# A PEER decoder layer: the second 128 sparse tokens' value rows added on VectorE, and the routing lookups summed over the innermost axis

## The chip, the cores and the metric

The kernel runs on one core of a Trainium2 chip. The metric is device time in microseconds (us) of one execution. A profiled execution gives the trace; its span runs from the first instruction to the last.

## The reference, cut to what matters

One layer over 512 tokens of width 1024. A token mixer comes first (projections, convolutions, pooling, attention, a layer norm); its output `x1` goes into a PEER expert mixer:

```python
q = (xf @ wq).reshape(t, 8, 2, 128)
scores = einsum("thpc,hpnc->thpn", q, sub_keys)
s_top, i_top = lax.top_k(scores, 16)
cand_s = s_top[:, :, 0, :, None] + s_top[:, :, 1, None, :]      # 16 x 16 sums
cand_i = i_top[:, :, 0, :, None] * 128 + i_top[:, :, 1, None, :]
best_s, best_pos = lax.top_k(cand_s, 16)
expert_idx = take_along_axis(cand_i, best_pos)                  # the lookups
act = gelu(einsum("cd,chkd->chk", x, u_tab[expert_idx])) * softmax(best_s)
out = einsum("chk,chkd->cd", act, v_tab[expert_idx])            # 128 rows a token
x = layer_norm(alpha * x + out)
```

Each token has 8 heads with 16 experts, so 128 rows of `u` and 128 rows of `v`, each row 1024 float32 numbers (4 KB). The tables have 16384 rows.

## The kernel before, in words

**Stages.** The mixer fills the first 200 us. Then comes the routing (`route_a` to `route_e`, to about 365 us): for each of 8 heads and two halves, `top16` finds the best 16 on VectorE, and two lookups turn a position among the candidates into the indices of the two halves. A lookup (`lookup`, L789) compares on VectorE (`ge`, float16, 1024 numbers a partition, the axes t, a, s) and multiplies on GpSimd by a difference (`pr`, the same axes); the 16 products of each output are then summed on VectorE. `add_up` (L797, called by `route_d`) sums the float32 products in one `tensor_reduce` whose innermost axis steps by 16 elements; `add_half` (L801, called by `route_e`) sums the float16 products in four `tensor_tensor` adds of halves (512, 256, 128 and 64 outputs). `route_d` and `route_e` work one and two iterations behind `route_c`, in the loop over `hp` (L865), and GpSimd's queue also holds the `wlo` subtractions (`split_w`, L118) that the next query projection on TensorE waits for. While VectorE ends the routing, TensorE works on blocks of the next stage (`ramp_fill`).

**The main loop** (L1267) treats the tokens in two ways. For the last 256 tokens ("dense") it goes through the whole tables, in 128 blocks of 128 experts. A block loads 512 KB of `uT` and 512 KB of `v`, splits each into a high and a low part (ScalarE copies, VectorE subtracts: `wlo`, `vl`), computes `h_run` (24 matmuls), multiplies by gates (`a_mul`, VectorE, L1004) and adds into `acc` (`v_tile`, 12 matmuls a block). The gates come as one-hot products (`g_hot` on VectorE, `g_token` on TensorE) in three windows of blocks, 14 to 31, 38 to 62 and 70 to 94 (`GWIN`), 16 groups in each.

For the first 256 tokens ("sparse", two groups of 128) it gathers rows by indirect DMAs that GpSimd issues (L1037), 128 rows of 4 KB (512 KB) at a time, into a ring of `NGAT` = 9 buffers named `gat`. A *u-row step* (`sparse_u`, L1040, one unit) holds row j of all 128 tokens of a group, a token on each partition, and makes one VectorE multiply with `accum_out`. A *V step* (`sparse_v`, L1097, four units) holds four gathers, in which the partitions are the 128 rows of one token, and makes eight matmuls of 512 columns with `expand` into `facc`; 32 such steps serve a group. The index tile is `idxs[i]` for u and its transpose `idxT` for v.

**Order.** The order of the sparse work is a list written by hand (L1164 to L1192), and `gq` holds the gathers in the same order. `work` (L1204) is called four times in a block and takes from the list by quotas: 5 units a block up to block 13, then 3.5, then about 4 from block 31. So the 128 u-row steps of group 0 run in blocks 0 to 30; then four u-row steps of group 1 alternate with one V step of group 0 (blocks 30 to 93); then group 0 is finished (`finish_a`, `finish_q`, `finish_0`, `finish_1`, block 94), and the 32 V steps of group 1 run, one a block, in blocks 94 to 125. What is left runs behind the loop, with `finish_a(128, ...)` and the last norms.

Each engine works in the order in which the program issues. In block b, TensorE does `h_run(b+1)`, then `v_tile(b)`; VectorE does the split for `b+2`, the split for `b+1`, the gate products, `a_mul(b+1)` (which waits for `h_run(b+1)`), `a_low(b+1)`, and the sparse steps in between. `v_tile(b+1)` waits for `a_low(b+1)`.

## Time and profile before

| | |
|---|---|
| median of 3 runs | 1426.06 us (1424.3 to 1428.26) |
| the profiled execution's own time | 1420.93 us |
| its span | 1419.1 us |
| mean granted TensorE clock | 0.977 |
| TensorE busy | 1322.5 us, 93% |
| VectorE busy | 1086.8 us, 77% |
| GpSimd busy | 779.0 us, 55% |
| ScalarE busy | 512.5 us, 36% |
| moved by DMA | 439.83 MB |

A busy share is a mean over stages with different limits, so the rows below cut the span into stages. PE is TensorE's matmuls, PEld its weight loads, DVE VectorE, ACT ScalarE, POOL GpSimd, SP the queue that issues plain loads. A tile's name is that of the program; a buffer is written left of `<-` and read right of it.

### The profile page before, as it was taken

Reading aid. Unit: us, or ns where it says so; the run is one execution under the profiler, and the core shown is the slowest. Engines: PE = TensorE matmul, PEld = TensorE weight load, DVE = VectorE, ACT = ScalarE, POOL = GpSimd, SP = SyncE. Lnnn points to the kernel's source line nnn. Section 1 sums busy time; section 2 is a strip of 40 time slices with the busy share of each in tenths; the row PEclk is TensorE's granted clock in tenths of the full one; section 3 lists DMA queues with packets and bytes.
Section 4 is the critical chain, followed back from the end, with each engine's and each line's share of the span. In section 5 each row is a group of like instructions: output and inputs, shape, how many; then the busy total and the mean of one; then the engine's idle time right before and its main releaser. Section 6 shows DMA issues by size and latency. Waiting matters only on the chain.

```text
span 1419.1 us, 24250 instructions
## 1 busy us (share of the span) xinstructions
PE 1322.5 (93%) x9229; PEld 1006.2 (71%) x9229; DVE 1086.8 (77%) x2292; ACT 512.5 (36%) x735; POOL 779.0 (55%) x687
## 2 busy tenths in 40 slices
PE   9999999989995668998999999999999989999996
PEld 6787889989862234666677777777778767777774
DVE  7876669999987899998788888778888843444445
ACT  4654524321420001323344434334444443333333
POOL 2242317774537786667666665666656545455450
PEclk9999999999998888999999999999999999999998
DMA  6520323223659999999999999999999999999993
GB/s 212 186 63 13 134 84 128 83 75 110 229 199 389 420 411 367 378 375 375 413 377 392 388 385 390 405 419 404 405 403 402 406 364 416 402 419 409 419 408 141
DMA packets 125444, 439.83 MB, mean 310 GB/s; under 512 B 14480, under 2 KB 16528, under 8 KB 125328
## 3 DMA queue, kind: packets, MB, share of 16 engines
q0 software_dynamic: 73728, 268.47, 48.0%
q1 hardware_dynamic: 51312, 168.78, 31.6%
q8 instruction: 72, 1.18, 0.3%
q10 hardware_dynamic: 288, 1.05, 0.2%
q14 instruction: 44, 0.36, 0.1%
HBM read 435.09 MB, written 3.15 MB: 309 GB/s over the span
## 4 chain that ended last, share of the span: by engine, by line
PE 50%; issue 14%; DMA 13%; POOL 11%; DVE 10%; ACT 2%; POOLq 0%; DVEq 0%; SPq 0%; ACTq 0%
PE acc L1253 12%; PE w L1261 11%; POOL gat L1037 10%; DMA gat<-in_v,idxT 8%; PE facc L1102 8%; DMA gat<-in_u,idx 4%; PE b L138 4%; PE b L139 4%; PE b L137 4%; PE w L703 3%; DVE i_top L757 2%; DVE s_top L755 1%; PE z L312 1%; DVE sc L760 1%; DVE gat L1042 1%
## 5 line engine op out<-in xcount | busy, mean ns | idle before, releaser
L1037 POOL DMA_INDIRECT gat<-in_u,idx x256 | 336.5, 1314 | 222.5 <-DVE gat L1042 142.6
L1037 POOL DMA_INDIRECT gat<-in_v,idxT x256 | 280.6, 1096 | 178.6 <-PE facc L1102 100.1
L1042 DVE SCALAR_TENSOR_TENSOR gat<-gat,x1s 128x1024 f32<-128x1024 f32 x256 | 309.4, 1222 | 15.7 <-DMA gat<-in_u,idx 15.1
L1253 PE MATMUL acc<-vh,A 128*128 128x512 f32 x768 | 261.5, 401 | 0.0
L1261 PE MATMUL w<-x1Tdh,whi 128*128 128x256 f32 x832 | 241.7, 291 | 1.6 <-ACT gl L1264 1.4
L1261 PE MATMUL w<-x1Tdl,whi 128*128 128x256 f32 x832 | 235.2, 283 | 0.0
L1261 PE MATMUL w<-x1Tdh,wlo 128*128 128x256 f32 x832 | 234.9, 282 | 0.0
L118 DVE TENSOR_TENSOR vl<-vraw,vh 128x1024 fp32r<-128x1024 f32 x96 | 117.5, 1224 | 121.2 <-ACT vh L115 121.1
L1253 PEld LDWEIGHTS acc<-vh,A 128*128 128x128 f32 x768 | 145.1, 189 | 81.5 <-issue 28.5
L1243 PE MATMUL acc<-vraw,af 128*128 128x512 f32 x248 | 136.9, 697 | 48.6 <-DVE af L1004 45.2
L115 ACT ACTIVATE whi<-wraw 128x1024 fp32r<-128x1024 f32 (+1 forms) x146 | 151.0, 1036 | 48.6 <-DMA wraw<-in_wq 25.5
L1102 PE MATMUL facc<-gat,expand 128*32 128x512 f32 x1024 | 152.5, 600 | 14.8 <-DMA gat<-in_v,idxT 14.1
L1261 PEld LDWEIGHTS w<-x1Tdh,whi 128*128 128x128 f32 x832 | 159.4, 192 | 6.1 <-ACT gl L1264 2.3
L1261 PEld LDWEIGHTS w<-x1Tdl,whi 128*128 128x128 f32 x832 | 159.3, 191 | 2.4
L1261 PEld LDWEIGHTS w<-x1Tdh,wlo 128*128 128x128 f32 x832 | 159.0, 191 | 0.0
L118 DVE TENSOR_TENSOR wlo<-wraw,whi 128x1024 fp32r<-128x1024 f32 (+1 forms) x109 | 131.7, 1210 | 34.7 <-ACT whi L115 34.0
L115 ACT ACTIVATE vh<-vraw 128x1024 fp32r<-128x1024 f32 x96 | 101.4, 1056 | 143.5 <-issue 118.1
L1253 PE MATMUL acc<-vl,A 128*128 128x512 f32 x384 | 151.0, 393 | 0.0
L118 POOL TENSOR_TENSOR wlo<-wraw,whi 128x1024 fp32r<-128x1024 f32 x37 | 92.5, 2504 | 96.0 <-ACT whi L115 96.0
L1243 PEld LDWEIGHTS acc<-vraw,af 128*128 128x128 f32 x248 | 51.1, 219 | 112.3 <-DVE af L1004 61.2
L115 ACT ACTIVATE ring<-w 128x384 f32<-128x384 f32 (+2 forms) x80 | 52.4, 740 | 169.4 <-PE w L973 169.4
L1264 ACT ACTIVATE gl<-w 128x256 f32<-128x256 f32 x104 | 39.9, 384 | 185.3 <-PE w L1261 182.8
(301 smaller groups left out, 2376.8 us busy)
## 6 DMA issues: line engine op xcount, KB each, us to landing
wraw<-in_uT SPq DMA_DIRECT2D x128, 512.0 KB, 8.4
vraw<-in_v SPq DMA_DIRECT2D x128, 512.0 KB, 6.5
wraw<-in_w_in SPq DMA_DIRECT2D x18, 512.0 KB, 3.8
wraw<-in_wq SPq DMA_DIRECT2D x16, 512.0 KB, 3.9
wo<-in_w_out SPq DMA_DIRECT2D x8, 512.0 KB, 9.3
gat<-in_u,idx POOLq DMA_INDIRECT x256, 8.3
gat<-in_v,idxT POOLq DMA_INDIRECT x256, 6.9
wo<-in_xT SPq DMA_DIRECT2D x8, 256.0 KB, 5.5
```

Of the source, the lines that this page charges most:

```text
L115: return act.activation(o, i, AF.Copy, scale=scale)
L118: eng.tensor_tensor(out=o, in0=a, in1=b, op=OP.subtract)
L137: pe.matmul(ps, lh, rh, start=start, stop=False)
L138: pe.matmul(ps, lh, rl, start=False, stop=False)
L139: pe.matmul(ps, ll, rh, start=False, stop=stop)
L703: pe.matmul(ramp[1], uraw[b][:, k, :], native["x"][:, k, :], start=k == 0, stop=k == 7)
L1037: pool.indirect_dma_start(out=t, out_offset=None, in_=table, in_offset=bass.IndirectOffsetOnAxis(ap=idx, axis=0))
L1042: dve.scalar_tensor_tensor(t, t, 1.0, x1s[i], op0=OP.mult, op1=OP.mult, accum_out=dots[:, j:j + 1])
L1102: pe.matmul(facc[hf][32 * j:32 * j + 32, :], expand[:, j, o:o + 32], ts[j][:, 512 * hf:512 * hf + 512], start=r == 0, stop=r == 31)
L1243: pe.matmul(acc[hf], af[b][:, c:c + 128], raw[:, 512 * hf:512 * hf + 512], start=b == 0, stop=False)
L1253: pe.matmul(acc[hf], lhs[x], rhs[y], start=b == 0 and p == 0, stop=b == NI - 1 and p == 2)
L1261: pe.matmul(ps, w[:, k, :], x1Td[x][:, k, :], start=k == 0 and p == 0, stop=k == 7 and p == 2)
```

## The change

Two things are changed together.

*Routing.* GpSimd writes its products `pr` through a rearranged view, so that the 16 products of one output lie side by side. Both lookups are then summed by one `tensor_reduce` over the innermost axis; `add_half` is gone.

*Main loop.* The V steps of group 1 and their eight matmuls are gone. In their place stand 128 *f steps* of one unit each: a gather of `v` with the same index column as for u (a token on each partition), and one VectorE multiply-add `x1s[1] = t * coef[:, j] + x1s[1]`, which reads and writes the same tile as the f step ahead of it. A ScalarE copy multiplies `x1s[1]` by alpha before the first; the last also writes the sum that the norm needs, so `finish_a(128, ...)` is gone. The list is rewritten: eight u-row steps of group 1, then one V step of group 0, 15 times over; then one V step and six f steps, 17 times over; then the end of group 0 with four f steps between its parts, and the last 22 f steps. The transposed indices of group 1 are no longer made.

```diff
-    idxT = mp.tile([128, SPT], I32, name="idxT")
+    idxT = mp.tile([128, 128], I32, name="idxT")
...
-            pool.tensor_tensor(out=pr, in0=ge, in1=delta[:, :, :, None].to_broadcast([128, NB, TOPK, TOPK]), op=OP.mult)
+            pool.tensor_tensor(out=pr.rearrange("p t s a -> p t a s"), in0=ge, in1=delta[:, :, :, None].to_broadcast([128, NB, TOPK, TOPK]), op=OP.mult)
...
-                dve.tensor_reduce(out=dst, in_=pr.rearrange("p t a s -> p t s a"), axis=AX.X, op=OP.add)
-
-        def add_half(dst, pr):
-            n = TOPK // 2
-            while n:
-                o = pr[:, :, :n] if n > 1 else dst[:, :, None]
-                dve.tensor_tensor(out=o, in0=pr[:, :, :n], in1=pr[:, :, n:2 * n], op=OP.add)
-                n //= 2
+                dve.tensor_reduce(out=dst, in_=pr, axis=AX.X, op=OP.add)
...
-            add_half(i2A[:, :, h, :], pr)
+            add_up(i2A[:, :, h, :], pr)
...
+        pe.transpose(eps_[:, :128], ef[:, 0, :], ident)
         for i in range(NU):
-            pe.transpose(eps_[:, 128 * i:128 * i + 128], ef[:, i, :], ident)
...
-            if kind not in "uv":
+            if kind not in "uvf":
                 continue
-            table, idx = (u, idxs[i][:, j:j + 1]) if kind == "u" else (v, idxT[:, 128 * i + j:128 * i + j + 1])
+            table = u if kind == "u" else v
+            idx = idxT[:, j:j + 1] if kind == "v" else idxs[i][:, j:j + 1]
...
+    def sparse_scale():
+        copy_act(x1s[1], x1s[1], scale=ALPHA)
+
+    def sparse_f(j):
+        t = gats.pop(("f", 1, j))
+        more = {}
+        if j == 127:
+            fs = mp2.tile([128, 4], F32, name="fs", bufs=4)
+            more["accum_out"] = fs[:, 0:1]
+            fin[128] = [x1s[1], fs[:, 2:3], fs[:, 3:4], x1s[1]]
+        dve.scalar_tensor_tensor(x1s[1], t, coef[:, j:j + 1], x1s[1], op0=OP.mult, op1=OP.add, **more)
+        if j == 127:
+            dve.tensor_scalar(fs[:, 2:3], fs[:, 0:1], -1.0 / D, None, op0=OP.mult)
+        held[0] -= 1
...
+    def add_f(n):
+        for j in range(nf[0], nf[0] + n):
+            gq.append(("f", 1, j))
+            sparse.append((1, lambda j=j: sparse_f(j)))
+        nf[0] += n
+
+    nf = [0]
     zero(sparse_act, 0)
     zero(sparse_clear)
-    for k in range(34):
-        if k < 32:
-            for j in range(4):
-                add_u(1, 4 * k + j)
...
-        if k > 1:
-            add_v(0, k - 2)
...
+    for k in range(16):
+        for j in range(8):
+            add_u(1, 8 * k + j)
+            if k == 0 and j == 0:
+                zero(sparse_turn)
+            if k == 0 and j == 4:
+                zero(sparse_expand, 0)
+        if k:
+            add_v(0, k - 1)
+    zero(sparse_act, 1)
+    zero(sparse_scale)
+    for r in range(15, 32):
+        add_v(0, r)
+        add_f(6)
...
     zero(finish_a, 0, facc, x1s[0])
-    zero(sparse_expand, 0)
+    add_f(2)
     sparse.append((1, lambda: finish_q(0)))
     zero(finish_0)
+    add_f(2)
     sparse.append((1, finish_1))
-    for k in range(32):
-        add_v(1, k)
+    add_f(128 - nf[0])
...
-    sparse.append((1, lambda: finish_a(128, facc, x1s[1])))
     sparse.append((1, lambda: finish_q(128)))
```

## Rows read from the trace of the kernel before

**Rows 1.** The page's first part: busy time, share, instructions of each engine.

```profile
PE 1322.5 (93%) x9229; PEld 1006.2 (71%) x9229; DVE 1086.8 (77%) x2292; ACT 512.5 (36%) x735; POOL 779.0 (55%) x687
```

**Rows 2.** Windows by stage: busy time of each engine, clock, DMA share, GB/s.

```profile
427.80:515.40 87.60, 52.54 (x89) 20.27 (x89) 71.89 (x126) 0.00 (x0) 69.61 (x60) 0.81 1.02 411
...
639.00:697.90 58.90, 50.56 (x278) 36.03 (x277) 47.08 (x73) 19.85 (x33) 39.17 (x31) 0.97 1.00 391
697.90:897.80 199.90, 196.32 (x1602) 152.02 (x1601) 166.59 (x257) 85.43 (x118) 126.56 (x101) 1.00 1.00 388
897.80:953.40 55.60, 52.71 (x321) 39.14 (x320) 42.06 (x64) 19.79 (x30) 34.07 (x30) 1.00 1.03 416
953.40:1149.40 196.00, 191.94 (x1622) 152.28 (x1624) 163.84 (x254) 85.85 (x136) 117.50 (x97) 1.00 1.02 404
1149.40:1178.90 29.50, 26.48 (x165) 17.42 (x161) 12.50 (x16) 12.13 (x19) 16.32 (x15) 1.00 0.94 365
1178.90:1393.60 214.70, 214.70 (x1460) 156.91 (x1456) 92.64 (x112) 78.78 (x115) 104.81 (x107) 1.00 1.02 408
```

**Rows 3.** The same windows for line 1004 alone, one instruction a block.

```profile
697.90:897.80 199.90, 10.50 (x25) 1.00 1.00 388
...
1178.90:1393.60 214.70, 11.90 (x28) 1.00 1.02 408
```

**Rows 4.** The chain of waits in one late block.

```profile
1177.82 1.85 PE facc L1102 x16
1179.67 2.95 PE acc L1253 x12
1182.62 2.87 PE w L1261 x24
```

**Rows 5.** Window of one block with four u-row steps and no gate group.

```profile
704.20:711.80 7.60, 7.60 (x78) 5.32 (x77) 7.45 (x12) 3.73 (x6) 3.92 (x4) 1.00 1.02 411
```

**Rows 6.** Timeline of VectorE: multiply-adds with a scalar per partition.

```profile
132.84 1.54 DVE L406 SCALAR_TENSOR_TENSOR h<-ut,cvc,h 128x512 f32<-128x512 f32 x2
...
178.22 1.28 DVE L605 SCALAR_TENSOR_TENSOR x1s<-bigl,sd,sp 128x1024 f32<-128x1024 f32 x1
```

**Rows 7.** Waits from 640 to 1149 us: us in total, times, longest.

```profile
PEld facc L1102 <- DMA gat<-in_v,idxT: 33.3, 33, 2.3
...
PE facc L1102 <- DMA gat<-in_v,idxT: 11.1, 14, 1.4
```

**Rows 8.** The routing's lookups by tile: ns min/median/max, first and last start.

```profile
L805 DVE TENSOR_TENSOR pr<-pr x24: 224/292/2400, 240.9 to 363.9; 128x512 f16<-128x512 f16 x8, 128x256 f16<-128x256 f16 x8, 128x128 f16<-128x128 f16 x8
L794 POOL TENSOR_TENSOR pr<-ge,dl x16: 1924/1932/1978, 228.4 to 360.8; 128x1024 f32<-128x1024 f16 x8, 128x1024 f16<-128x1024 f16 x8
L799 DVE TENSOR_REDUCE pki<-pr x8: 1878/1910/1973, 232.8 to 357.5; 128x64 int32<-128x1024 f32 x8
...
L805 DVE TENSOR_TENSOR i2A<-pr x8: 224/224/2320, 241.9 to 364.2; 128x64 f32<-128x64 f16 x8
...
L908 DVE TENSOR_REDUCE sm<-sc x1: 678/678/678, 360.5 to 360.5; 128x32 f32<-128x512 f32 x1
```

**Rows 9.** Groups of instructions over the span: busy us, mean ns, idle before.

```profile
L1042 DVE SCALAR_TENSOR_TENSOR gat<-gat,x1s 128x1024 f32<-128x1024 f32 x256 | 309.4, 1222 | 15.7 <-DMA gat<-in_u,idx 15.1 <-DVE gat L1042 0.4
...
L805 DVE TENSOR_TENSOR pr<-pr 128x512 f16<-128x512 f16 (+2 forms) x24 | 13.5, 563 | 0.5
```

**Rows 10.** Windows of the routing loop and of its end.

```profile
227.00:324.70 97.70, 90.78 (x766) 89.33 (x766) 96.43 (x542) 29.69 (x42) 69.19 (x92) 1.00 0.27 88
324.70:360.30 35.60, 35.60 (x186) 31.90 (x185) 35.05 (x187) 8.19 (x17) 16.09 (x31) 1.00 0.37 119
```

**Rows 11.** Waits from 225 to 365 us.

```profile
PE b L139 <- POOL wlo L118: 3.7, 3, 1.7
...
PE b L745 <- ACT qs L115: 3.1, 2, 1.6
```

More of the change, by code (lines that the diff above doesn't have):

```diff
@@ L929, in hybrid_kernel @@
         ramp_fill(TFILL[3])
-        dve.tensor_copy(idxT, eps_[:, :SPT])
+        dve.tensor_copy(idxT, eps_[:, :128])
     pctx.close()
@@ L1162, in add_v @@
         sparse.append((4, lambda: sparse_v(i, r)))
+    def add_f(n):
[4 more added lines that the diff above has]
+    nf = [0]
     zero(sparse_act, 0)
     zero(sparse_clear)
-    for k in range(34):
-        if k < 32:
-            for j in range(4):
-                add_u(1, 4 * k + j)
-        if k == 0:
-            zero(sparse_turn)
-        if k == 1:
-            zero(sparse_expand, 0)
-        if k == 32:
-            zero(sparse_act, 1)
-        if k > 1:
-            add_v(0, k - 2)
-        if k == 32:
-            zero(sparse_turn)
+    for k in range(16):
[12 more added lines that the diff above has]
+        add_f(6)
     gq.append(("s", 0, 0))
@@ L1182, in hybrid_kernel @@
     zero(finish_a, 0, facc, x1s[0])
-    zero(sparse_expand, 0)
+    add_f(2)
     sparse.append((1, lambda: finish_q(0)))
     zero(finish_0)
+    add_f(2)
     sparse.append((1, finish_1))
-    for k in range(32):
-        add_v(1, k)
+    add_f(128 - nf[0])
     gq.extend(("l", i, 1) for i in range(2))
     gq.extend(("x", i, 0) for i in range(2))
-    sparse.append((1, lambda: finish_a(128, facc, x1s[1])))
     sparse.append((1, lambda: finish_q(128)))
```

## Prediction

> **What bounds the kernel now.** I read the page's shares first [rows 1]: TensorE at 93%, VectorE at 77%. These are means over stages, so I cut the loop with windows at block boundaries [rows 2] and counted blocks by `a_mul`, one a block [rows 3].
>
> Late stage (blocks 98 to 125, V steps only): 214.7 us for 28 blocks, 7.67 each, TensorE busy throughout. The chain of waits shows the same block in three pieces, 1.85 (V) + 2.95 (`acc`) + 2.87 (`h_run`) = 7.67 [rows 4]. DMA is close: four gathers and two loads of 512 KB are 3.146 MB a block, and at the best rate of these windows, 416 GB/s, take 7.56 us. VectorE has 92.64 / 28 = 3.31 us of work a block. So two limits nearly coincide, and VectorE idles.
>
> Second gate window (blocks 38 to 62): 199.9 / 25 = 8.00 us a block at 388 GB/s, slower than either limit. TensorE shows 196.32 us busy, but part of that is standing still: from 640 to 1149 us its V steps wait 33.3 us (weight loads) and 11.1 us (matmuls) for gathers [rows 7]. A V step that waits stops TensorE, since its queue is in order. Blocks 70 to 94 are like it (196.0 us), and at the end of group 0 (95 to 97) three blocks take 29.5 us at 365 GB/s, 6.5 more than three late ones.
>
> Routing: from 227 to 324.7 us VectorE is busy 96.43 of 97.7, TensorE 90.78; then, to 360.3, TensorE is busy all 35.6 us [rows 10]. VectorE sets the pace first, TensorE behind it.
>
> **The routing's part.** Removed: eight strided reduces of 1.91, and 32 adds. 24 of these cost 13.5 us [rows 9]; their median is 0.292, but single ones reach 2.40; the last eight are 0.22 each with one of 2.32 [rows 8], about 3.9. Added: eight more reduces, sixteen in all, contiguous. A contiguous reduce of 512 float32 took 0.678, and elementwise instructions go from about that to 1.22 at 1024 [rows 8, 9], so I take 1.21. Bounds: 0.68 (if float16 went at double rate) and 1.91 (if nothing improves). Saved on VectorE: 8 x (1.91 - 1.21) = 5.6, and 13.5 + 3.9 - 8 x 1.21 = 7.7; together 13.3 us.
>
> The rows show four adds costing 17.4 / 8 = 2.2 us on average although their medians are short, whereas the one-input reduces stay within 1.88 and 1.97 [rows 8, 9]. The Trainium skill speaks against the swap in "VectorE: DVE Perf Modes", The perf-mode tier table: 16-bit `tensor_tensor` reaches double rate, `tensor_reduce` only single. By that alone the swap of the adds would save nothing and the routing 5.6. But "SBUF — State Buffer", Who interferes with whom, says that an instruction with two SBUF inputs blocks against a GpSimd instruction that reads SBUF, and that a reduce never does; the spread of the adds agrees, and by it the 13.3 stands.
>
> Not all of it shortens the path. TensorE's order is fixed, and behind 324.7 it has no idle time; it can gain at most the 97.7 - 90.78 = 6.9 us that it idles before, of which 3.7 are waits for GpSimd's `wlo` and 3.1 for ScalarE's `qs` [rows 10, 11], both behind VectorE's pace. I take 5, between 0 and 7. The shorter `idxT` and the transpose left out hide behind TensorE's fills: nothing.
>
> GpSimd's product keeps its size but writes with a step of 16. No row has such a write on GpSimd. Below: 1.93 unchanged [rows 8]. Above: the strided reduce on VectorE costs 1.91 against 1.21, a factor of 1.58, so 3.05. I take a little above the lower end, since GpSimd's elementwise rate is slow already (1.93 for what VectorE does in 1.2): hidden in the 28.5 us that GpSimd idles of 97.7 [rows 10].
>
> **The loop's part.** Removed: 32 V steps of 1.85, 59 us of TensorE. Added: 128 f steps on VectorE. A 1024-wide multiply-add with a scalar per partition took 1.28, and two in place on one tile 1.54 for two of 512, 0.77 each, against 0.68 for a free one, so a dependent one gains nothing by overlap [rows 6, 8]. I take 1.3 a step; below 1.04 (a u-row step, from (7.45 - 3.31) / 4 [rows 2, 5]), above 1.54 (two of 512 in place). Gathers stay the same in number and size. An f step waits for its gather; behind it in VectorE's queue stand the splits and `a_mul`, and for those TensorE waits, but about a block later, where a V step stops TensorE at once.
>
> A gate group costs VectorE (166.6 - 25 x 3.31 - 50 x 1.04) / 16 = 2.0 us. With the new list, VectorE's work by stage against DMA's 7.56 a block, and what I take:
> - Blocks 31 to 37, u-row steps mainly: DMA 53; take 55 (now 58.9).
> - 38 to 62, 66 u-row steps for 50, 8 V steps for 12: VectorE 82.8 + 32 + 68.6 = 183, DMA 189; take 195 (now 199.9), as a third of the V steps that waited is gone and a late u-row step stops only VectorE, which runs ahead.
> - 63 to 69: DMA 53; take 54 (now 55.6).
> - 70 to 94, 18 u-row and 42 f steps: VectorE 82.8 + 32 + 18.7 + 54.6 = 188, DMA 189. Two limits meet again; take 197 (now 196).
> - 95 to 97: no end of group 0 here any more; take 23 (now 29.5).
> - 98 to 119, 55 f steps: VectorE 144, DMA 166; take 167 (now 168.7).
> - 120 to 125, 23 f steps and the end of group 0 (about 4 us on VectorE): 6 x 3.31 + 23 x 1.3 + 4 = 54, over DMA's 45; take 54 (now 46). VectorE becomes the bound here.
> - Behind the loop two f steps, 2.6, replace two half-row adds, 1.36: +1.2.
>
> Sum of the loop: -3.9 - 4.9 - 1.6 + 1 - 6.5 - 1.7 + 8 + 1.2 = -8.4. With the routing -13.4. From the profiled execution's 1420.93 (span 1419.1, 1.8 around it) that is 1407.5; the median of the runs lies 5.1 above it, so 1413. The `coef` product, which waits for ScalarE, only moves from block 92 to 77; ScalarE's copy behind it is one more instruction on an engine busy 36% [rows 1], and VectorE's first f step stands in the next block: nothing, about 1 us if VectorE should be waiting there.
>
> **The rivals.**
>
> *Forecast, chance 0.5:* both gains, 1413; its own range 1400 to 1421.
>
> *The gathers keep the pace, 0.2.* For it: 1.00 to 1.03 DMA share everywhere, and nine buffers still hold both kinds of steps. Then blocks 31 to 69 stay as they are (10.4 of the gain lost) and the rest gives -5 + 2: about 1423. Against it: the windows with only u-row steps ran at 411 GB/s, so a waiting VectorE can fill the queues.
>
> *VectorE becomes the bound of the second half, 0.2; slower.* The f steps wait for each other and for their gathers, on the engine that is now fullest. The price of one f step decides: at 1.8 us blocks 70 to 94 take 209, 98 to 119 172, 120 to 125 65 and the tail 1 more, 29 us in all, and the time is 1442; the gain is gone at 1.63. For it: in-place pairs at 0.77 per 512. Against it: 256 u-row steps idled only 15.7 us for their gathers, at 1.22 each [rows 9].
>
> *GpSimd's strided product is slow, 0.1.* At 3.05, sixteen of them add 18 us to GpSimd, `wlo` comes later, TensorE's wait for it (3.7, [rows 11]) grows, and the routing gains nothing: 1418, or some us more. "GPSIMD Engine Reference" of the Trainium skill, Performance pitfalls for Q7 kernels, puts about half more on reads with a step over 8 bytes, which would make 2.9 us of 1.93; it says nothing of writes, and no run here shows one.
>
> **Numbers.** A measurement tells about 0.3%, 4.3 us, from no change: 1421.8 to 1430.3 is "same". Faster: 0.46 of the forecast, 0.05 of the second case, 0.06 of the last: 0.57. Same: 0.04 + 0.13 + 0.02 + 0.03 = 0.22. Slower: 0.21. The range reaches from both gains full, with the loop at its limits (1398), to the lower part of the slower case (1437).
>
> **What would show it.** Right: f steps near 1.3 us; contiguous reduces near 1.2, both kinds; main loop beginning about 5 us earlier; blocks 38 to 62 below 8 us each; blocks 120 to 125 at 9 with VectorE full; TensorE's waits for gathers fewer. Wrong: f steps over 1.6, products on GpSimd near 3, VectorE full while GB/s falls below 390, or an unchanged start of the loop.

## The result and the profile after

The changed kernel is slower, by about 0.65%. Its median is 1436.15 us (1424.49 to 1445.96 in 20 runs) against 1425.55 us (1420.45 to 1431.41 in 20 runs) for the kernel before on the same chip: ratio 1.0065, 95% interval 1.0049 to 1.0081. Ratios, here and below, leave out single runs in a slower state (one of the changed kernel, one of `e3`) and are not exactly the quotients of the medians. The forecast was 1413 us; the time lies just inside the upper edge of the range (1437), and on the other side of the kernel before. The profiled execution took 1439.43 us with a span of 1437.7. That span is 18.6 us longer than the profiled one of before (1419.1), while the medians are 10.6 us apart, so a comparison of these two traces alone shows too much.

The shares, and then the stages in the same form as [rows 2] (window in us; length, then busy time and instruction count of TensorE, its weight loads, VectorE, ScalarE and GpSimd; clock, DMA share, GB/s). The stages are blocks 38 to 62, 63 to 69, 70 to 94, 95 to 97, 98 to 119 and 120 to 125. After them, in the same view, come three single blocks of the second gate window (42, 43, 44) and two late ones (116, 117).

```profile
PE 1301.1 (91%) x8715; PEld 999.3 (70%) x8715; DVE 1220.3 (85%) x2393; ACT 508.7 (35%) x731; POOL 857.9 (60%) x687
```

```profile
697.20:902.70 205.50, 195.01 (x1546) 151.60 (x1545) 183.77 (x291) 84.97 (x117) 138.76 (x102) 1.00 1.00 384
902.70:959.90 57.20, 53.47 (x313) 41.43 (x312) 47.64 (x73) 19.35 (x28) 35.45 (x29) 0.97 1.01 398
959.90:1162.80 202.90, 189.28 (x1547) 148.27 (x1545) 181.86 (x242) 85.24 (x135) 125.66 (x100) 0.99 1.00 386
1162.80:1188.20 25.40, 23.82 (x140) 17.19 (x141) 17.73 (x21) 8.32 (x12) 17.24 (x15) 1.00 1.02 414
1188.20:1364.30 176.10, 162.77 (x944) 121.97 (x943) 133.99 (x143) 60.85 (x88) 103.42 (x85) 0.98 1.00 396
1364.30:1413.30 49.00, 38.66 (x224) 32.11 (x223) 48.57 (x56) 19.70 (x29) 29.83 (x21) 0.97 0.99 378
...
730.40:738.00 7.60, 7.60 (x73) 6.78 (x72) 7.60 (x14) 3.74 (x5) 4.61 (x4) 1.00 0.99 368
738.00:747.80 9.80, 8.85 (x64) 5.07 (x63) 9.77 (x19) 3.72 (x5) 6.04 (x5) 1.00 1.02 412
747.80:754.80 7.00, 7.00 (x57) 6.31 (x56) 5.41 (x10) 2.81 (x4) 5.78 (x5) 1.00 0.95 345
1328.00:1335.90 7.90, 7.88 (x46) 6.65 (x45) 7.83 (x8) 2.81 (x4) 4.64 (x4) 1.00 1.02 411
1335.90:1349.30 13.40, 10.07 (x43) 4.49 (x44) 5.46 (x7) 2.69 (x4) 6.13 (x6) 0.87 1.02 411
```

VectorE's own work in blocks 38 to 62 is 183.8 us, as forecast (183), and yet the stage takes 205.5. The single blocks show why this sum does not bound the stage. Blocks 42 and 43 hold four u-row steps each, and VectorE is full in them (7.60 of 7.60, 9.77 of 9.80); block 44 holds a V step and no VectorE step, and there VectorE works 5.41 of 7.00 us. The time that is missing in one block is not made up in the next. The kernel before shows the same pair, a block with four u-row steps and a gate group, then one with a V step:

```profile
719.00:728.80 9.80, 9.14 (x66) 5.75 (x65) 9.77 (x16) 2.75 (x4) 3.68 (x4) 1.00 1.01 408
728.80:736.00 7.20, 7.20 (x71) 6.40 (x70) 3.32 (x7) 3.82 (x5) 5.76 (x5) 1.00 0.96 338
```

Before, one block in two of this stage was of VectorE's kind; now it is two in three.

The waits that answer to [rows 7] (640 to 1149 us, the first two lines) and to [rows 11] (225.8 to 361.5 us; the columns are the total in us, the times, the longest):

```profile
PEld facc L1111 <- DMA gat<-in_v,idxT: 56.9, 37, 2.4
PE facc L1111 <- DMA gat<-in_v,idxT: 25.1, 30, 1.5
...
DVE i2A L799 <- POOL pr L794: 5.7, 6, 1.8
...
PE b L139 <- POOL wlo L118: 5.0, 3, 2.2
```

TensorE's V steps wait longer for gathers in that stretch, although there are fewer of them: 56.9 us against 33.3 at the weight loads, 25.1 against 11.1 at the matmuls. (The two rows overlap, as one stop shows in both, so they are not to be added.) In the routing VectorE now waits for GpSimd's products, and TensorE waits longer for `wlo` (5.0, was 3.7). The groups of instructions that answer to [rows 8] (GpSimd and VectorE from 225 to 365 us), and the f steps (1030 to 1440 us):

```profile
L794 POOL TENSOR_TENSOR pr<-ge,dl 128x1024 f16<-128x1024 f16 x8 | 37.0, 4624 | 0.7 <-DVE ge L791 0.7
...
L794 POOL TENSOR_TENSOR pr<-ge,dl 128x1024 f32<-128x1024 f16 x8 | 16.0, 1996 | 18.2 <-DVE ge L791 18.2
...
L799 DVE TENSOR_REDUCE i2A<-pr 128x64 f32<-128x1024 f16 x8 | 9.7, 1218 | 5.7 <-POOL pr L794 5.7
L799 DVE TENSOR_REDUCE pki<-pr 128x64 int32<-128x1024 f32 x8 | 9.6, 1201 | 0.0
...
L1101 DVE SCALAR_TENSOR_TENSOR x1s<-gat,coef,x1s 128x1024 f32<-128x1024 f32 x128 | 163.9, 1280 | 0.9
```

The reduces (1.20 and 1.22 us) and the f steps (1.28) came out as priced. The products did not: in float32 1.996 us, hardly more than the 1.93 of [rows 8], in float16 4.62.

Last, block 117, the longest late one. GpSimd's timeline of the gathers that it issues (in brackets its idle time before, and what ended it), and the first piece of the chain of waits from 1335 to 1350 us:

```profile
1313.89 1.86 POOL L1031 DMA_INDIRECT gat<-in_v,idxT  x1 [5.41 <-DVE x1s L1101]
1316.06 1.22 POOL L1031 DMA_INDIRECT gat<-in_v,idx  x1 [0.30 <-issue]
...
1328.16 1.11 POOL L1031 DMA_INDIRECT gat<-in_v,idxT  x1 [0.30 <-issue]
1329.92 0.94 POOL L1031 DMA_INDIRECT gat<-in_v,idxT  x1 [0.65 <-DVE x1s L1101]
...
1344.57 0.93 POOL L1031 DMA_INDIRECT gat<-in_v,idx  x1 [4.73 <-PE facc L1111]
```

```profile
1329.92 12.40 DMA gat<-in_v,idxT
```

GpSimd stands 5.41 us for a buffer that an f step holds, then sends eleven gathers in 17 us (1313.89 to 1329.92), and the last of these, a V step's fourth, needs 12.40 us until its rows have landed. TensorE stands for it. Over the whole stretch (1188.2 to 1364.3 us) a V step's gather lands after 9.0 us, in the same stretch of the kernel before (1178.3 to 1347.0) after 6.9; first the kernel after, then before (instructions, median us from issue to landing):

```profile
gat<-in_v,idxT POOLq DMA_INDIRECT x31, 9.0
```

```profile
gat<-in_v,idxT POOLq DMA_INDIRECT x88, 6.9
```

The waits of the same two stretches, again first after, then before. `POOL gat` is GpSimd standing for a free buffer: all for V steps before, mostly for f steps now. The kernel before has no row of V steps waiting for gathers there.

```profile
POOL gat L1031 <- DVE x1s L1101: 40.4, 22, 7.5
PEld facc L1111 <- DMA gat<-in_v,idxT: 27.4, 17, 2.8
```

```profile
POOL gat L1037 <- PE facc L1102: 62.1, 22, 3.7
```

### The profile page after: what moved, and what is told of

Read it like the earlier page. It is cut to its first block, busy times and chain, and to the rows that moved or that the text cites. A ratio compares the mean times of both kernels' runs of the same rounds, so it can differ in the third digit from the quotient of the medians.

```text
span 1437.7 us, 23430 instructions
## 1 busy us (share of the span) xinstructions
PE 1301.1 (91%) x8715; PEld 999.3 (70%) x8715; DVE 1220.3 (85%) x2393; ACT 508.7 (35%) x731; POOL 857.9 (60%) x687
## 3 DMA queue, kind: packets, MB, share of 16 engines
q10 hardware_dynamic: 288, 1.05, 0.2%
## 4 chain that ended last, share of the span: by engine, by line
PE 26%; DMA 21%; issue 19%; POOL 19%; DVE 13%; ACT 1%; POOLq 0%; DVEq 0%; SPq 0%; ACTq 0%
POOL gat L1031 16%; DMA gat<-in_v,idxT 15%; DMA gat<-in_u,idx 4%; PE b L138 4%; PE b L139 4%; PE b L137 4%; PE facc L1111 3%; DVE gat L1036 3%; PE w L703 3%; DVE x1s L1101 3%; PE acc L1268 2%; PE w L1276 2%; POOL pr L794 2%; DVE ohB L950 1%; DMA gat<-in_v,idx 1%
## 5 line engine op out<-in xcount | busy, mean ns | idle before, releaser
L1031 POOL DMA_INDIRECT gat<-in_u,idx x256 | 343.8, 1343 | 174.8 <-issue 55.9
L1031 POOL DMA_INDIRECT gat<-in_v,idx x128 | 170.6, 1333 | 104.9 <-DVE x1s L1101 50.7
L1031 POOL DMA_INDIRECT gat<-in_v,idxT x128 | 161.1, 1259 | 87.4 <-DVE gat L1036 29.6
L1268 PEld LDWEIGHTS acc<-vh,A 128*128 128x128 f32 x768 | 145.5, 190 | 61.9 <-issue 18.9
L1101 DVE SCALAR_TENSOR_TENSOR x1s<-gat,coef,x1s 128x1024 f32<-128x1024 f32 x128 | 163.9, 1280 | 0.9
L1111 PE MATMUL facc<-gat,expand 128*32 128x512 f32 x512 | 124.4, 638 | 41.4 <-DMA gat<-in_v,idxT 41.3
L115 ACT ACTIVATE A<-af 128x256 fp32r<-128x256 f32 x97 | 40.5, 418 | 261.0 <-DVE af L997 261.0
```

The lines of the kernel that those rows point to most:

```text
L115: return act.activation(o, i, AF.Copy, scale=scale)
L1031: pool.indirect_dma_start(out=t, out_offset=None, in_=table, in_offset=bass.IndirectOffsetOnAxis(ap=idx, axis=0))
L1101: dve.scalar_tensor_tensor(x1s[1], t, coef[:, j:j + 1], x1s[1], op0=OP.mult, op1=OP.add, **more)
L1111: pe.matmul(facc[hf][32 * j:32 * j + 32, :], expand[:, j, o:o + 32], ts[j][:, 512 * hf:512 * hf + 512], start=r == 0, stop=r == 31)
L1268: pe.matmul(acc[hf], lhs[x], rhs[y], start=b == 0 and p == 0, stop=b == NI - 1 and p == 2)
```

## The experiments

All ratios are to the kernel before in runs on the same chip. The median of the kernel before lay between 1425.2 and 1434.2 us on the five chips of these runs, so compare ratios rather than times between groups.

### The two parts alone

`e1`: the loop before, the routing's part alone. `e2`: the same, but with float32 products for the second lookup too (the flags `ge` are float16 in every run, so what is said below of float32 flags has no counterpart in the code):

```
-            return lookup(bf, rankc, dl[:, 1], F16)
+            return lookup(bf, rankc, dl[:, 1])
```

`e3`: the loop's part alone, with the routing of before.

> The loop of the kernel before with the routing's part of the change alone. Theory (what the shorter reduces saved, GpSimd's float16 product gave back: 4.65 us against 1.93, eight of them): the main loop begins at 411 to 412 us, as in both kernels, and the time is within 2 us of the kernel before, 1424 to 1428. Rival 1 (the prediction's gain of 5 us is there, and the loop lost more than it seems): the loop begins near 406 and the time is about 1420. Rival 2 (the routing's part makes the whole kernel slower): about 1436.

> The loop of the kernel before with the routing's part, but the second lookup's product and flags in float32 as in the first. Theory (only the float16 product with a step of 32 bytes is slow, the float32 one is not): all sixteen products near 2.0 us, GpSimd's work in the routing falls back to about 70 us, TensorE's wait for wlo to 3 us or less, the loop begins near 406 and the time is about 1420. Rival (TensorE has no idle time there that could be taken away): products near 2.0, but the loop begins at 411 and the time stays at 1425. Rival 2: VectorE pays for float32 flags (the comparison writes twice the bytes) and nothing is won.

> The loop's part of the change alone, with the routing of the kernel before. Theory (all of the loss lies in the loop): 1434 to 1438, the loop beginning at 411. Rival (the two parts work on each other, or the routing lost too): nearer to 1426 to 1430.

| run | median us | ratio | 95% interval |
|---|---|---|---|
| e1 routing's part alone | 1428.35 | 1.0018 | 0.9998 to 1.0037 |
| e2 with float32 products | 1416.29 | 0.9925 | 0.9896 to 0.9955 |
| e3 loop's part alone | 1437.44 | 1.0064 | 1.0035 to 1.0092 |

The loss is the loop's. The routing's part gives nothing, and with float32 products it gives 0.75%, about 10 us. In `e2` the products (groups, 225 to 365 us), TensorE's wait for `wlo` (same stretch) and the first `a_mul` of the loop (by tile; the two times are the first and the last start) are:

```profile
L794 POOL TENSOR_TENSOR pr<-ge,dl 128x1024 f32<-128x1024 f16 x16 | 31.8, 1988 | 23.3 <-DVE ge L791 23.3
```

```profile
PE b L139 <- POOL wlo L118: 0.4, 1, 0.4
```

```profile
L997 DVE SCALAR_TENSOR_TENSOR af<-ring x16: 418/421/475, 404.3 to 516.4; 128x256 f32<-128x256 f32 x16
```

The loop begins at 404.3 us there, in the kernel before at 411.2, in the changed one at 411.9 and in `e1` at 414.9. As `e2` differs from `e1` in the type of these eight products alone, the float16 product is what stood between the reduces and their gain.

### The gathers of the V steps earlier (e4)

```
+    placed = []
+    for e in gq:
+        if e[0] == "v":
+            if e[2] < 32:
+                lead = {"u": 4, "f": 3}.get(placed[-1][0], 0)
+                at = len(placed) - lead if e[2] not in (0, 15) else len(placed)
+            placed.insert(at, e)
+            at += 1
+        else:
+            placed.append(e)
+    gq.clear()
+    gq.extend(placed)
```

> The changed kernel with the same steps in the same order, but the four gathers of a V step stand ahead of the last four u-row or the last three f gathers of the group before them, so that the steps run in the old order and only the gathers change places. Theory A (a V step's gathers are issued late, because they wait for buffers that f or u-row steps on VectorE still hold): TensorE's waits for gathers from 1030 to 1360 us fall to a half or less, blocks 98 to 119 take about 7.6 us instead of 8.0, and the time falls by 8 to 12 us, to 1424 to 1428. Theory B (VectorE itself is the bound, the gathers only follow it): no change, 1436; V steps wait less, but TensorE waits for VectorE's splits instead.

1445.82 us, ratio 1.0123 (1.0078 to 1.0167): both theories are wrong. Over the whole loop the V steps do wait less: in the rows of the tile `facc`, weight loads and matmuls taken together, TensorE's idle time for gathers falls from 131.6 to 57.4 us, and blocks 38 to 62 took 197.2 us where the changed kernel took 205.5. But from 1030 to 1360 us it hardly falls (weight loads 37.9 to 30.0, matmuls 17.6 to 16.9), and now the f steps wait, 47.5 us in the first row below (waits, 1030 to 1360 us), where in the changed kernel VectorE was idle 0.9 us before all its f steps.

```profile
DVE x1s L1101 <- DMA gat<-in_v,idx: 47.5, 16, 7.5
...
PEld facc L1111 <- DMA gat<-in_v,idxT: 30.0, 16, 3.0
```

Which step waits is settled by the order of the gathers; that some step waits was not cured by this order. A V step's four buffers that are filled earlier are held longer.

### Steps spread evenly (e5, e6), and eight buffers (e7, e8)

`e5` and `e6` keep the order of steps and gathers and the step with which each stage begins. Inside a stage every step counts one, so a block takes two or three steps, of both kinds:

```
+    ends, costs = (0, 14, 31, 38, 63, 70, 95, 98, 120, NI - GLAST), [c for c, _ in sparse if c]
+    cum, n = [0], 0
+    for end in ends[1:]:
+        while n < len(costs) and sum(costs[:n]) < sum(quota[:end]):
+            n += 1
+        cum.append(n)
+    quota = []
+    for (b0, n0), (b1, n1) in zip(zip(ends, cum), zip(ends[1:], cum[1:])):
+        quota += [(n1 - n0) * (k + 1) // (b1 - b0) - (n1 - n0) * k // (b1 - b0) for k in range(b1 - b0)]
...
-            debt[0] -= used
+            debt[0] -= min(used, 1)
```

`e7` and `e8` are the two kernels with `NGAT = 8`.

> The changed kernel, same steps and gathers in the same order, each stage beginning with the same step as before, but within a stage the steps are spread evenly over the blocks: a V step counts one like the others, so that a block takes two u-row or f steps and a V step, or three, and not four of one kind and then a V step alone. Theory C (a block takes the larger of VectorE's and TensorE's work, and the change put more blocks with four VectorE steps in place of V blocks: 9.83 us with a gate group, 7.58 without, against 7.2 for a V block): blocks 38 to 62 fall from about 204 to about 193 us, 70 to 94 from about 202 to about 194, 98 to 119 to about 168, and the time falls by 15 to 22 us, to 1414 to 1421. Rival D (the gathers come late however the steps are spread, as nine buffers turn over at the same rate): V and f steps wait for gathers instead, and the time stays within 4 us of 1436.

> The same even spreading in the kernel before: five steps in two blocks (four u-row, one V) as two and three, not four and one; late stage one V step a block as it was. Theory C: the kernel before alternates blocks too (9.84 and 7.2), so blocks 38 to 62 fall from 200 to about 192 and 70 to 94 from 196 to about 191, the time to about 1412 to 1416, and the distance to the changed kernel made even is what is left of the change. Rival D: unchanged at 1426.

> The changed kernel with eight gather buffers instead of nine. Theory D (the turnover of the buffers sets the pace, more so behind the change, since f steps hold them too): slower by 20 us or more, and by at least 10 us more than the kernel before with eight. Theory C: slower, but by about as much as the kernel before with eight.

> The kernel before with eight gather buffers instead of nine. Theory D: slower by some us, up to 10, as a V step's four buffers are released at once and the gathers of the next can be issued together. Theory C: slower by about as much as the changed kernel with eight.

| run | median us | ratio | 95% interval |
|---|---|---|---|
| e5 changed, even | 1419.88 | 0.9956 | 0.9933 to 0.9978 |
| e6 before, even | 1414.74 | 0.9916 | 0.9891 to 0.9942 |
| e7 changed, eight buffers | 1474.20 | 1.0333 | 1.0308 to 1.0358 |
| e8 before, eight buffers | 1453.32 | 1.0202 | 1.0171 to 1.0233 |

Both times with even steps came as theory C said, and D's "unchanged" fell. The stages came out less well than the sums: in the profile of `e5` blocks 38 to 62 took 208.1 us, not 193, with two blocks of 16.2 and 13.2 in which TensorE stood for gathers, and `e6` kept blocks 70 to 94 at 207.9, not 191. So these two times agree with theory C, but their profiles do not show its mechanism. The eight buffers told little apart: the changed kernel lost 2.7% (1.0333 / 1.0065) and the kernel before 2.0%, so both hang on the buffers, the changed one by some 9 us more (uncertain by 6), where D wanted 10 or more and C none; D's "up to 10" for the kernel before fell (28).

### Gathers of half a row (e9 to e12)

The four kernels (changed and before, steps in fours and even) with half the bytes in each gather. Every step still works on 1024 columns, the same 512 twice:

```
-            pool.indirect_dma_start(out=t, out_offset=None, in_=table,
+            pool.indirect_dma_start(out=t[:, 512:], out_offset=None, in_=table.rearrange('r (a c) -> (r a) c', c=512),
...
+    def twice(t):
+        return t[:, None, 512:].to_broadcast([128, 2, 512])
...
-        dve.scalar_tensor_tensor(x1s[1], t, coef[:, j:j + 1], x1s[1], op0=OP.mult, op1=OP.add, **more)
+        dve.scalar_tensor_tensor(x1s[1], twice(t), coef[:, j:j + 1], x1s[1], op0=OP.mult, op1=OP.add, **more)
```

> The changed kernel with gathers of half a row: each gather fetches 512 of the 1024 columns (256 KB, not 512), and the u-row, f and V steps read these 512 twice, so that every step costs its engine what it did and only the transfers are smaller; the output is another. It shows what the loop takes when DMA's rate is no limit: at 409 GB/s a block's transfers take 5.1 us. Theory C (a block takes the larger of VectorE's and TensorE's own work): blocks of four VectorE steps stay at 7.6 to 7.9, with a gate group at 9.8, so blocks 38 to 62 stay near 200 and 70 to 94 near 198; only the waits of V steps (41 us of TensorE in the profile of the changed kernel) go; 1405 to 1415. Rival D (the turnover of the gathers alone sets the pace): both windows fall under 190, the whole to 1390 or less, below the kernel before with half gathers.

> The kernel before with gathers of half a row, as above (the steps read the fetched half twice; the output is another). Theory C: blocks 98 to 125 stay at 7.67, as TensorE is full there; 38 to 62 fall little, to about 195, since a block of four u-row steps is VectorE's (7.58, with a gate group 9.84) and a V block TensorE's; 31 to 37, 63 to 69 and 95 to 97 fall by some 10 us together; 1405 to 1412, and the distance to the changed kernel shrinks to 0 to 5. Rival D: the distance turns round, the kernel before is the slower one by 10 us or more, having 59 us more work on TensorE.

> The changed kernel with gathers of half a row (as above, another output) and steps spread evenly. Theory C: with neither DMA nor alternation in the way the work of the engines is all that is left: 38 to 62 near 7.5 a block, 70 to 94 near 7.5 (VectorE), 98 to 119 near 6.6, 120 to 125 8.2 (VectorE): about 1385, clearly below the changed kernel with half gathers (1405 to 1415). Rival D: evenness adds nothing once the gathers are cheap; the same as the changed kernel with half gathers within 4 us.

> The kernel before with gathers of half a row (another output) and steps spread evenly. Theory C: 98 to 125 stay at 7.67 a block (TensorE), 38 to 62 about 7.4, about 1398, now slower than the changed kernel in the same form, as the work taken from TensorE counts once neither DMA nor alternation is in the way. Rival D: the same as without the even spreading, within 4 us.

| run | median us | ratio | 95% interval |
|---|---|---|---|
| e9 changed, half gathers | 1404.01 | 0.9797 | 0.9768 to 0.9827 |
| e10 before, half gathers | 1408.97 | 0.9823 | 0.9774 to 0.9871 |
| e11 changed, half, even | 1382.39 | 0.9638 | 0.9601 to 0.9675 |
| e12 before, half, even | 1396.88 | 0.9749 | 0.9717 to 0.9782 |

Theory C's four times hold within 3 us; the distance between `e9` and `e10`, which it put at 0 to 5 us, came out as 5 us the other way, and two stages of `e9` missed it: blocks 38 to 62 took 193.8 us (near 200 expected), 70 to 94 took 208.4 (near 198). What the change does in each setting is the quotient of two ratios:

| | whole gathers | half gathers |
|---|---|---|
| steps in fours | 1.0065 | 0.9797 / 0.9823 = 0.9974 |
| steps even | 0.9956 / 0.9916 = 1.0040 | 0.9638 / 0.9749 = 0.9886 |

By the intervals above, each entry is uncertain by 0.002 to 0.006. So taking away one of the two, the whole gathers or the fours, does not turn the change into a clear gain. With both taken away it gains 1.1%, some 15 us. The two do not weigh the same. Half gathers move the change's effect by 0.009 (fours) and 0.015 (even); even steps move it by 0.0025 with whole gathers, which is within the uncertainty, and by 0.009 with half ones, which is barely outside. The gathers are the larger part of what the change loses. The windows of blocks 38 to 62, 70 to 94 and 98 to 119, `e9` first and then `e10`:

```profile
693.40:887.20 193.80, 184.33 (x1533) 150.13 (x1532) 183.08 (x291) 83.34 (x117) 145.27 (x100) 0.99 0.80 266
939.10:1147.50 208.40, 190.31 (x1567) 151.20 (x1567) 181.75 (x242) 84.30 (x135) 131.60 (x101) 0.97 0.76 252
1170.40:1324.40 154.00, 152.75 (x944) 121.62 (x944) 133.75 (x142) 60.76 (x89) 110.46 (x85) 1.00 0.87 298
```

```profile
696.00:892.50 196.50, 189.95 (x1600) 151.96 (x1599) 166.01 (x258) 84.35 (x117) 134.01 (x99) 0.99 0.78 262
946.00:1139.10 193.10, 187.22 (x1617) 150.33 (x1619) 163.65 (x255) 85.30 (x135) 122.63 (x97) 1.00 0.81 274
1166.40:1333.60 167.20, 167.20 (x1136) 122.77 (x1138) 73.00 (x89) 62.15 (x90) 97.17 (x88) 1.00 0.84 276
```

In blocks 38 to 62 the changed kernel is now 2.7 us shorter, where with whole gathers it was 5.6 us longer (205.5 against 199.9). Two blocks in three are still VectorE's there, so alternation costs time (VectorE works 183.1 of 193.8 us), but in this stage it is not what makes the change lose.

In blocks 70 to 94 the changed kernel is still 15 us longer, with DMA at 0.76 of its time: that is not the gathers, for which its V steps wait 2.9 us at the weight loads and 1.1 at the matmuls. TensorE waits for ScalarE instead. A gate group's matmuls wait until ScalarE has copied the group before it into `ring`, and in ScalarE's queue that copy stands behind the copy of `af`, for which ScalarE waits while VectorE is full. The waits for `ring` in this stage (total, times, longest), `e9` first and then `e10`:

```profile
PE w L965 <- ACT ring L115: 16.8, 8, 2.8
```

```profile
PE w L972 <- ACT ring L115: 3.4, 6, 1.1
```

Behind the gate stages the changed kernel is 13 us shorter (154.0 against 167.2), with TensorE all but full in both: this is the relief that the prediction counted on, and with whole gathers (176.1 in the changed kernel) it is gone.

### Where the even steps help (e13, e14)

The edit of `e5` for blocks 38 to 94 alone (`e13`), and from block 95 on alone (`e14`):

```
-            debt[0] -= used
+            debt[0] -= min(used, 1) if 38 <= b < 95 else used
```

> The changed kernel with the steps spread evenly in blocks 38 to 94 alone; from 95 on in groups of four as in the changed kernel. Theory C (alternation of VectorE's and TensorE's blocks in the gate stages is the larger part of the loss): 8 to 12 us below the changed kernel, 1424 to 1428. Theory D (late gathers behind block 95 are the larger part): within 4 us of the changed kernel, 1432 to 1436.

> The changed kernel with the steps spread evenly from block 95 on alone; before that in groups of four as in the changed kernel. Theory D: blocks 98 to 119 take about 167 us instead of 176, 8 to 12 us below the changed kernel, 1424 to 1428. Theory C: 4 us or less below it, 1432 to 1436.

`e13` takes 1426.21 us, ratio 0.9959 (0.9937 to 0.9981), as much as even steps everywhere (0.9956); `e14` takes 1437.96, ratio 1.0054 (1.0033 to 1.0076), as good as nothing. So what even steps give lies in the gate stages. Three blocks of `e13` (42 to 44), with the same eight u-row steps, one V step and two gate groups as the three of the changed kernel above, and its stages 38 to 62 and 70 to 94:

```profile
733.50:738.90 5.40, 3.63 (x39) 3.41 (x38) 5.36 (x11) 3.64 (x5) 4.49 (x4) 1.00 0.92 323
738.90:748.00 9.10, 9.10 (x69) 8.07 (x68) 8.76 (x15) 3.84 (x5) 7.57 (x6) 1.00 1.01 391
748.00:756.70 8.70, 7.67 (x77) 5.71 (x76) 8.67 (x17) 2.70 (x4) 4.94 (x4) 1.00 1.03 418
...
700.50:895.50 195.00, 189.16 (x1539) 151.87 (x1535) 182.23 (x289) 85.12 (x116) 134.02 (x95) 1.00 0.99 383
955.60:1154.10 198.50, 188.30 (x1578) 153.18 (x1577) 181.73 (x246) 85.31 (x135) 129.89 (x103) 0.99 1.01 399
```

VectorE does the same 22.8 us in the three blocks of both kernels (7.60 + 9.77 + 5.41; 5.36 + 8.76 + 8.67), but they take 24.4 us in fours and 23.2 spread, and VectorE idles 0.4 us in place of 1.6. The V steps also wait less for gathers in `e13`, from 640 to 1149 us 44.2 us at the weight loads and 18.9 at the matmuls (56.9 and 25.1 in the changed kernel), so `e13` by itself does not tell alternation from gathers; `e9` and `e11`, in which gathers are small, show that even steps also help without them.

### Fewer steps beside a gate group, and the best version (e15 to e18)

`e15` and `e16` also give a block with a gate group less room for steps, with the float32 products of `e2`; `e17` and `e18` have the plain spreading of `e5` and `e6` with these products.

```
+    gated = {lo + (hi - lo) * tg // NG for lo, hi in GWIN for tg in range(NG)}
...
+        room = [42 - 22 * (k + 1 in gated) for k in range(b0, b1)]
+        quota += [(n1 - n0) * sum(room[:k + 1]) // sum(room) - (n1 - n0) * sum(room[:k]) // sum(room) for k in range(b1 - b0)]
```

> The loop of the kernel before, spread evenly and with fewer steps in a block with a gate group (2.0 us of room for steps instead of 4.2), and the routing's part with float32 products. From e2 (10 us) and e6 (10.5 us) alone: 1405. If the gate groups make the alternation: blocks 38 to 62 and 70 to 94 at 7.6, some 7 us more, about 1398. If not: 1405.

> The changed kernel, spread evenly and with fewer steps in a block with a gate group, and float32 products in the routing. From e2 and e5 alone: 1410. If the gate groups make the alternation: about 1402. It stays behind the kernel before in the same form (e15) if the late gathers go on costing what the relieved TensorE gives.

> The loop of the kernel before with the plain even spreading of e6 and the routing's part with float32 products of e2. If the two gains add up (ratios 0.9916 and 0.9925) the ratio is 0.984, about 1403, and the gate-aware spreading of e15 cost 5 us. If they do not, 0.988 as in e15.

> The changed kernel with the plain even spreading of e5 and float32 products in the routing. If the gains add up (0.9956, and 0.0075 for the products) 0.988, about 1409, and the gate-aware spreading of e16 cost 9 us. If they do not, 0.994 as in e16. In both cases 4 to 6 us behind e17.

| run | median us | ratio | 95% interval |
|---|---|---|---|
| e15 before, gate-aware, float32 | 1411.91 | 0.9880 | 0.9856 to 0.9904 |
| e16 changed, gate-aware, float32 | 1421.49 | 0.9944 | 0.9911 to 0.9978 |
| e17 before, even, float32 | 1410.55 | 0.9833 | 0.9802 to 0.9864 |
| e18 changed, even, float32 | 1417.88 | 0.9893 | 0.9861 to 0.9925 |

The gains of `e2` and `e6` add up (0.9925 x 0.9916 = 0.9842 against 0.9833). The gate-aware spreading costs 0.5% in both kernels, against what I expected; why, no run shows. `e17` is the best of those with the right output: 1.7% faster than the kernel before, and of the change it keeps only the contiguous reduces, with float32 products. `e18` against `e17` (0.9893 / 0.9833 = 1.0061, uncertain by 0.0045) shows once more that with whole gathers the loop's part loses some 0.5% with even steps too.

## Why the prediction was wrong, step by step

**The routing's 5 us.** The prices of the reduces were right (1.20 and 1.22 for 1.21 forecast; the sixteen take 9.7 + 9.6 = 19.3 us, 13.4 less than before, for 13.3 forecast), and so was the step that TensorE could gain what it waits for `wlo`: `e2` takes that wait from 3.7 to 0.4 us, and its loop begins 6.9 us earlier. The failing step is the price of GpSimd's product, "a little above the lower end". It holds for float32 (1.996) and not for float16 (4.62, far above the upper bound of 3.05). The last rival named this engine and this place, but applied one price to all sixteen, taken from a float32 read on VectorE. By the eight float16 products GpSimd works 8 x (4.62 - 1.93) = 21.5 us more, and `e1` shows the result: no gain. The rule of the Trainium skill that the rival cited ("GPSIMD Engine Reference", Performance pitfalls for Q7 kernels: half more for reads with a step over 8 bytes) does not cover these writes, and neither size agrees with it: float32 with a step of 64 bytes pays 3%, float16 with a step of 32 bytes 140%. The reduces agree with "VectorE: DVE Perf Modes" of the Trainium skill, The perf-mode tier table, by which a `tensor_reduce` has only the single rate: 1.22 us from float16 and 1.20 from float32.

**The loop's gathers.** "Gathers stay the same in number and size", and so their cost was put at nothing; the waits of V steps were to become fewer, "as a third of the V steps that waited is gone". This is the step that costs the change its gain. From 640 to 1149 us the V steps' waits rose from 33.3 to 56.9 us (weight loads), and in blocks 98 to 119 from none to 27.4. With half gathers the change's effect goes from a loss of 0.65% to 0.26% on the other side (uncertain by 0.6), and with even steps as well to a gain of 1.1%. The forecast's own rival, that the gathers keep the pace, was the nearest; it expected the waits to stay, and a small gain (1423). Blocks 31 to 37 and 63 to 69, forecast at 55 and 54, close to DMA's best rate, took 58.4 and 57.2. Half gathers make each transfer shorter and DMA's total smaller at once, so they do not tell the turnover of the nine buffers from DMA's rate; that eight buffers cost the changed kernel some 9 us more than the kernel before (uncertain by 6) speaks for the turnover.

**Blocks 38 to 62 and 70 to 94, forecast at -4.9 and +1, came out at +5.6 and +6.9.** The stages were bounded by sums over 25 blocks, VectorE's 183 and 188 and DMA's 189, on the ground that "a late u-row step stops only VectorE, which runs ahead". It does not run ahead: four VectorE steps in one block fill VectorE there, and in the next it waits for TensorE. The three-block rows of the changed kernel and of `e13` show it. In blocks 70 to 94 of `e9` VectorE's lateness reaches TensorE through ScalarE (the waits for `ring`), without gathers in the way. Putting the steps of the changed kernel evenly into these stages gains 1.06% (1.0065 - 0.9959, uncertain by 0.3), while the waits for gathers fell too. But the kernel before pays for its fours too (`e6`, 0.84%), so of the change's own 0.65% even steps take away only about 0.25, which the intervals do not tell from nothing. In blocks 38 to 62, with the steps still in fours, half gathers bring the stage below that of before (193.8 against 196.5), and so do other places for the gathers (`e4`, 197.2 against 199.9). So alternation is a cost that the sums left out, but with whole gathers it is not shown to be what the change adds.

The windows of several profiles, to show how far one may be trusted (us; blocks 98 to 119 of `e13` have the order of the changed kernel):

| blocks | before | e1 | e2 | changed | e3 | e14 | e13 |
|---|---|---|---|---|---|---|---|
| 38 to 62 | 199.9 | 199.1 | 200.3 | 205.5 | 202.8 | 207.1 | 195.0 (even) |
| 70 to 94 | 196.0 | 199.1 | 196.2 | 202.9 | 200.8 | 211.2 | 198.5 (even) |
| 98 to 119 | 168.7 | 168.7 | 168.7 | 176.1 | 169.0 | 171.4 (even) | 166.4 |

**Blocks 98 to 119, forecast at 167.** They took 176.1 in the profile, but 169.0 and 166.4 in two others with the same order, so against the 168.7 of before the change brings something between a loss of some 8 us and a gain of 2, and not the gain of 13 that half gathers show. The forecast took DMA's best rate as a floor that is reached. In the profile of the changed kernel it is not: the stretch ran at 396 GB/s. `e3` and `e13` came nearer:

```profile
1185.80:1354.80 169.00, 158.86 (x944) 121.75 (x943) 134.04 (x142) 60.84 (x88) 104.47 (x86) 1.00 1.02 409
```

```profile
1179.90:1346.30 166.40, 157.05 (x936) 118.72 (x933) 130.54 (x141) 60.83 (x88) 105.94 (x87) 0.99 1.02 413
```

Nine buffers pass in order from f steps on VectorE to V steps on TensorE; each holds up the other's gathers (GpSimd stood 40.4 us for f steps), these go out in bursts, and a V step's last one can land late (12.40 us in block 117). Before, all nine served V steps alone, and the median landing was 6.9. The part of this that is shown: with half gathers the loss turns into a gain, and moving the gathers only moves the wait (`e4`). That more buffers would cure it is only argued: ten do not fit into SBUF beside the program's other tiles, so no run has them; eight cost 2 to 2.7%. TensorE's granted clock was 0.98 in this stretch and 1.00 before, so up to some 3 us of the 176.1 (2% of the 162.8 us in which it worked, an estimate) may be the lower clock; no run separates that.

**Blocks 120 to 125, forecast at 54, took 49.0; 95 to 97 at 23, took 25.4.** The f step was priced by its row, 1.3, and its row is 1.28. The rows of all VectorE instructions in blocks 120 to 125 add up to 53.8 us, as forecast; but VectorE was busy only 48.57, because an instruction begins before the row of the one ahead has ended. In block 116 the next one starts 1.19 us after an f step of 1.28. Two f steps in a row overlap by nothing (2.59 for both), as the prediction said of dependent ones:

```profile
1328.38 1.28 DVE L1101 SCALAR_TENSOR_TENSOR x1s<-gat,coef,x1s 128x1024 f32<-128x1024 f32 x1
1329.57 0.42 DVE L118 TENSOR_TENSOR A<-af,A 128x256 fp32r<-128x256 f32 x1
...
1333.44 2.59 DVE L1101 SCALAR_TENSOR_TENSOR x1s<-gat,coef,x1s 128x1024 f32<-128x1024 f32 x2
```

"Perfetto Trace Analysis" of the Trainium skill, Optimizing Scalar/DVE Operations, says that an instruction's write acknowledgement, a part of its profiled time, overlaps with the next instruction; the 0.09 us between different instructions agrees with it, the two f steps in a row do not show it. The same overlap makes VectorE's work in blocks 70 to 94 and 98 to 119 smaller than forecast (181.9 for 188, 134.0 for 144). So VectorE is the bound in blocks 120 to 125, as forecast, but at 8.2 us a block and not at 9. The rival in which VectorE bounds the second half came near in time (1442) by a wrong price, which is luck: it needed 1.63 us a step for the gain to go and 1.8 for its 1442.

**What held:** reduces, f steps, VectorE's work in blocks 38 to 62 (183.8 for 183), the end of group 0 moving away from block 95 (29.5 to 25.4). **What decided:** the gain of the loop was a small difference between TensorE's relief and its new costs, taken from sums in which neither late gathers nor alternation stands.

## What to carry to other kernels

In a loop whose engines cannot run ahead of each other, as here, add up the time of the fuller engine block by block; the larger of the engines' sums over a stage is too low a bound. Before moving work from one engine to another, look at single blocks for one engine full and the other idle in turn, and spread the steps first: here that gained more (0.84%) than the moved work did. Follow a late engine through every queue that waits for it, not only to the engine that it feeds. When steps of two engines share one ring of buffers, the release of one engine's step times the other's transfers: test with smaller transfers whether the relief of an engine can show at all. Price a changed layout for each element type apart, on the engine that writes it and not only on the one that reads it.

## What the runs showed of the hardware

- A GpSimd multiply that writes 1024 numbers a partition with a step of 16 elements took 4.62 us in float16 and 1.996 us in float32; contiguous, both took 1.93 [rows 8]. Only the float16 write is slow.
- VectorE's reduce over the innermost axis took 1.20 us contiguous against 1.91 with a step of 16 float32 [rows 8].
- In VectorE's packed blocks an instruction started about 0.09 us before the row of the one ahead ended (1.19 us after an f step of 1.28), but two dependent f steps in a row took 2.59 us.
- In block 117, where TensorE stood for gathers, the granted clock is 0.87 in the mean, so part of it ran at the lower of the two levels (1.2 GHz): cut finer, it is 0.54 from 1342.3 to 1345.7 us, after TensorE had worked 1.05 us of 3.7, and 1.00 again from 1345.7. The other single blocks shown show 1.00.
